# A hybrid mixer layer on one core: where the second pair's up-projection weights are prepared, which operand is finished first, and which PSUM banks the first two pairs use

## The chip, the cores and the metric

The kernel runs on one core of a Trainium2 chip. The metric is the device time of one execution in microseconds. The core has a matrix engine (PE; its weight loads are listed apart as PEld), a vector engine (DVE), a scalar engine (ACT), a general engine (POOL), which here mostly issues transfers, and a sync engine (SP), which issues transfers only. They run side by side, each through its own list of instructions in a fixed order, and wait for one another by semaphores. Matrix products are accumulated in PSUM, in banks of 512 fp32 columns; DVE and ACT read them from there.

## The reference

One layer is computed for 512 sample tokens and 128 prompt tokens, 640 in all: four token mixers with gates, an output projection, and a gated feed-forward network with a convolution over neighbouring tokens. The change concerns the step from the output projection to the network's up projection:

```
x = x + g1 * (merged @ w_o)
h = rmsnorm(x, norm2_g) * (1.0 + sc2) + sh2
x = x + g2 * conv_ffn(h, ...)

def conv_ffn(h, w_up, cw, cb, w_down):
    z = dwconv3(h @ w_up, cw, cb)
    a, g = jnp.split(z, 2, axis=-1)
    return (jax.nn.silu(g) * a) @ w_down
```

`h` is 640 x 1024, `w_up` is 1024 x 5632, `w_down` is 2816 x 1024.

## The kernel before

Every fp32 product is made of three matmuls in a faster 32-bit format. An operand x is split into a high half (ACT copies x, which rounds it) and a low half (DVE subtracts the high half from x); the product is high x high + high x low + low x high.

**The up loop.** The 5632 output columns are 22 pairs of 128 + 128 (the two halves of the gated unit). Tokens are split into two halves of 320 (`HC`), the 1024 features into two of 512. Each pair is thus a 2 x 2 block product, done in Winograd's form with seven block products in place of eight. A block product, `prod`, is twelve matmuls (4 k-tiles x 3) of 320 columns. Products are numbered 1 to 7. Each has an operand on the token side (1, 2 and 4 are blocks of h; 3, 5, 6 and 7 are sums and differences of blocks) and one on the weight side. The weight side of a pair lies in three "units": A for products 1 and 2 (plain blocks of the weight), B for 5 and 6 and the high half of 7, C for 3 and 4 and the low half of 7. B and C hold sums of weight blocks (`up_sums`, four sums of 512 columns) and one plain block, all split into high and low (`up_b`, `up_bl`, `up_c`).

`up_pair` is the loop's body. Step p runs products 6, 5 and 7 of pair p, products 4 and 3 of pair p-1, and for pairs from 4 on products 1 and 2 of pair p (`up_start`). ACT and DVE take the results out of PSUM, apply the convolution (`centre`: one ACT instruction; `taps`: two DVE multiply-adds of 641 columns), the gate, and POOL stores the result. They also prepare the weights of the next pair. For the first four pairs (`BRIDGE`) products 1 and 2 run ahead of the loop, as they need the plain blocks of h alone; meanwhile the last tokens are normalised and the sums of blocks made (`operands`).

**The passage before it.** The output projection `wo_tile(nh, kk_, w)` has two halves of 512 columns; in the first (nh = 0) four k-steps accumulate five token tiles in five banks `wo["acc"]`; in the second (nh = 1) each token tile is finished in turn, and `norm2(t)` starts: square sum on ACT, scaling on DVE, and after a delay eight transposes on PE, whose results ACT and DVE bring into the blocks of h (regions XH, XL0, XL1, X0). `up_early` runs beside the projection as a background job: it loads weight blocks of the first four pairs into regions that are free until norm2 needs them, makes unit A of pairs 0 to 3 and units B and C of pair 0, and writes those whose place is wanted later to a scratch tensor `upd` in memory. `up_back` reads them back (POOL issues it) when the projection's operands are done. Pair 1's units B and C are made in the passage itself, at step 0 of the loop.

**What sets the order.** Background jobs are Python generators. `tick` adds the planned PE time of the matmuls traced so far to a clock, and a job goes on when the time it yielded has passed (`UE`, `HD`: planned microseconds). This gives a program order. A scheduler then orders each engine's list by that priority and by when it believes the operands ready; it may put a ready instruction ahead of one that is not. `tc.keep_in_program_order` pins an instruction behind the one traced before it on the same engine. `ovec`, `oact` and `opool` pin all that goes through them while `fixed[0]` is set, which is so inside the loop (their rows carry line 148). Matmuls of the loop are not pinned.

**Where tiles live.** `region(tag, ...)` gives a named place in SBUF, used by one tile after another; the next user waits for the last access of the one before. `wp` and `rp` are rings of three places. `pg()` gives a PSUM tile of two banks (two such tiles), `pm()` one of a single bank (four). In the loop each pair's two accumulators `up[p_, "b"]` are the two halves of one `pg()` tile; pairs 2 and 3 use `pm()`.

Of the kernel before, what the change touches and what calls it, by code (L numbers as in the profile page):

```python
# [38 lines left out]
m17LH m07HL m15HL m17HL m16LH m14HH m24HL m26HL m27LH  # L39
""".split()  # L40
WARM = 100
UE = [5, 3]
NPL = 2
LOWD = ("ac", "ax", "ab", "d")
T = 640
# [22 lines left out]
def tile_step(ctx: ExitStack, tc: tile.TileContext, a: dict, outs: list, dbg=None):  # L68
# [1157 lines left out]
    def wo_tile(nh, kk_, w):  # L1226
        if (nh, kk_) == (0, 0):
            start(up_early(), 1)
            drain(lambda: "ada39" in R)
            grows["g1"] = gain_load(0, "F")  # L1230
            xr0 = region("X0", [P, 2560])
            xr1 = region("X1", [P, 2560])
            xr2 = region("G", [P, 1280])
            x2.extend([xr0[:, 0:1024], xr0[:, 1024:2048], xr1[:, 0:1024], xr1[:, 1024:2048],
                       xr2[:, 0:1024]])
            for t in range(5):
                pool.dma_start(x2[t], xsrc[t])
            g0, g1, m0 = pg(), pg(), pm()
            wo["acc"] = [m0, g0[:, 0, :], g0[:, 1, :], g1[:, 0, :], g1[:, 1, :]]
        wo[kk_] = w  # L1240
        if nh == 1 and kk_ < 3:
            return
        for t in range(5):
            m = pm() if nh == 1 else wo["acc"][t]
            for q in (range(4) if nh == 1 else (kk_,)):
                for k in (2 * q, 2 * q + 1):
                    for i, (hx, hw) in enumerate(((0, 0), (0, 1), (1, 0))):
                        mm(m, mh[k // 2][:, hx, k % 2, t * P:(t + 1) * P], wo[q][:, hw, k % 2, :],  # L1248
                           start=(k == 0 and i == 0), stop=(k == 7 and i == 2))
                    tick(0.65)  # L1250
            if kk_ < 3:
                continue
            v = 0 if t < 4 else 1
            tmp = gp.tile([P, 512], F32, tag="gt", name=nm("wt"))
            cs = slice(nh * 512, nh * 512 + 512)
            vec.tensor_tensor(tmp, m, grows["g1"][:, v, cs], ALU.mult)
# [11 lines left out]
    def norm2(t):  # L1268
# [9 lines left out]
        vec.tensor_scalar(xn, x2[t], st2[:, 8 + t:9 + t], None, ALU.mult)  # L1278
# [82 lines left out]

    upd = dram.tile([4, P, 5, 4, P], F32, name="upd")

    def up_early():
        x = region("XH", [P, 5, 8, P])
        ra, r1, r2 = x[:, 0], x[:, 3], x[:, 4]
        r3 = region("XL1", [P, 8, P])
        rb = region("H", [P, 8, P])  # L1370
        for r, p_, h in ((r2, 2, 0), (r3, 3, 0), (ra, 0, 0), (rb, 0, 1), (r1, 1, 0)):
            nc.sync.dma_start(r, a["w_up"][p_, h].rearrange("p a b c -> p (a b) c"))
        flat = lambda v: v.rearrange("p a b c -> p (a b) c")

        def part(hi, lo, v):
            act(hi, v, AF.Copy)
# [12 lines left out]
        s = x[:, 1:3].rearrange("p a b c -> p (a b) c")  # L1389
        b11, b21, b22, b12 = ra[:, 0:4], ra[:, 4:8], rb[:, 0:4], rb[:, 4:8]  # L1390
        q = [s[:, 4 * i:4 * i + 4] for i in range(4)]
        vec.tensor_tensor(q[0], b11, b12, ALU.add)
        vec.tensor_tensor(q[1], q[0], b22, ALU.add)
        vec.tensor_tensor(q[2], b12, b22, ALU.add)
        yield UE[1]
        vec.tensor_tensor(q[3], q[1], b21, ALU.add)
        b, c = [region(t, [P, 5, 4, P], F32R) for t in ("XL1", "XL0")]
        part(flat(b[:, 0:2]), flat(b[:, 2:4]), s[:, 0:8])
        part(b[:, 4], c[:, 4], q[2])
        nc.sync.dma_start(upd[2], b.bitcast(F32))  # L1400
        yield UE[1]
        for i, v in enumerate((q[3], b22)):
            part(c[:, i], c[:, 2 + i], v)
        nc.sync.dma_start(upd[3], c.bitcast(F32))
        R["early"] = True

    def up_back(p_, u, w, i, n):
        up[p_, u] = w
        pool.dma_start(w[:, 0:n], upd[i][:, 0:n])

    def up_sums(p_, r, part):
        s = sums(p_)
# [27 lines left out]
    def prod(o, p_, i, first, part=None):  # L1440

        u, ih, il = PROD[i]
        wh = up[p_, u][:, ih]
        wl = up[p_, "C" if i == 7 else u][:, il]
        xh_, xl_ = fx["x"][i]
        for k in range(4) if part is not None else ():
            for j, (w, x) in enumerate(((wl, xh_),) if part else ((wh, xh_), (wh, xl_))):
                mm(o, w[:, k, :], x[:, k, :], start=(first and not part and k == 0 and j == 0),
                   stop=(part == 1 and k == 3), skip_group_check=True)
                tick(0.147)  # L1450
        for k in range(4) if part is None else ():
            for j, (w, x) in enumerate(((wh, xh_), (wh, xl_), (wl, xh_))):
                mm(o, w[:, k, :], x[:, k, :], start=(first and k == 0 and j == 0),  # L1453
                   stop=(k == 3 and j == 2), skip_group_check=True)
            tick(0.44)

    def up_start(p_):

        if p_ == 2 or p_ == 3:
            up[p_, "b"] = [pm()[:, 0:HC], None]  # L1460
        else:
            g = pg()
            up[p_, "b"] = [g[:, 0, 0:HC], g[:, 1, 0:HC]]
        if p_ >= BRIDGE:
# [73 lines left out]
    def up_u2(p_):  # L1538

        if up[p_, "b"][1] is None:  # L1540
            up[p_, "b"][1] = pm()[:, 0:HC]
        b1 = up[p_, "b"][0]
        prod(b1, p_, 6, False)
        oact(tmp(p_ % 2), b1, AF.Copy)

    def up_pair(p_, r):
# [3 lines left out]
        inner, nx = p_ < NPAIR, n < NPAIR  # L1550
        if p_ == 0:
            up_u2(p_)
            up_sums(n, r[n], 0)
            up_sums(n, r[n], 1)
            operand3()
        if o >= 0:
            taps(o, 1)
        if q >= 0:

            oact(tmp(2), up[q, "b"][0], AF.Copy)  # L1560
            for (i0, i1, c) in S2:
                ovec.tensor_tensor(ubuf(q, 1)[:, c:c + i1 - i0], up[q, "b"][1][:, i0:i1], tmp(2)[:, i0:i1],
                                  ALU.subtract)
# [25 lines left out]
        if q >= 0:  # L1589
# [7 lines left out]
            if p_ == 1:  # L1597
                first_copy(3)
                first_sum(3)
        if inner and p_:  # L1600
# [5 lines left out]
        if nx:  # L1606
            up_b(n)
        if q >= 0:
            centre(q, 1)
        if nx:  # L1610
            up_bl(n)
        if inner:
            b1, b2 = up[p_, "b"]
# [3 lines left out]
    def operands(c0, c1):  # L1617

        if "t" not in fx:
            fx["t"] = region("X1", [P, 2, 4, HC])  # L1620
# [6 lines left out]
        def split(w, x, dma=False):  # L1627
            w = w[:, :, :, c0:c1]
            oact(w[:, 0], x, AF.Copy)
            if dma:  # L1630
                low_dma(w[:, 1], x)
            else:
                ovec.tensor_tensor(w[:, 1], x, w[:, 0].bitcast(F32), ALU.subtract)
# [512 lines left out]
```

## Time and profile before

| | |
|---|---|
| time before, median of 3 runs | 1030.13 us (1029.94 to 1030.38) |
| the profiled execution's own time | 1029.45 us |
| its span, first to last instruction | 1027.7 us |
| granted TensorE clock, mean | 0.998 |
| PE busy | 1013.2 us, 99% |
| DVE busy | 789.9 us, 77% |
| ACT busy | 537.3 us, 52% |
| POOL busy | 109.1 us, 11% |
| output projection, first and last matmul's start | 534.5 us, 591.8 us |
| products 1 and 2 of pairs 0 to 3 | 591.8 to 607.7 us |
| up loop, first product 6 | 607.7 us |

A row of the profile in order of time gives the start, the length, the engine, the line, the operation, the tile written <- the tiles read with their shapes, the count, and in brackets how long the engine was idle before and what ended it. Tile names are those of the regions: A, B and D hold operands 6, 5 and 7; E and w (the ring) hold unit B of an even and an odd pair; C and w hold unit C; XL is XL0 or XL1; g is a half of a two-bank PSUM tile, m a one-bank tile. Matmuls are pipelined: a row of twelve is 1.92 us long, but the next begins 1.76 us after it. The chain of waits lists only such steps.

### The profile page before, as it was taken

What the parts mean: (1) busy time and instruction counts of PE and PEld (TensorE: products, weight loads), DVE (VectorE), ACT (ScalarE), POOL (GpSimd) and SP (SyncE); (2) the same over time, 40 slices, a digit from 0 to 9 for tenths busy, and PEclk for the clock granted to TensorE, in tenths of its full rate; (3) what the DMA queues carried; (4) which work ended last, traced back from release to release, by engine and by line L of the source; (5) the groups of instructions that cost most, each with busy time, mean ns of one, the idle gap of its engine ahead of it and who ended that gap; (6) DMA issues with size and microseconds to landing.
All of it is one profiled execution on the core that took longest, in us unless ns stands there. A gap on an engine that the chain in (4) does not pass through costs nothing.

```text
span 1027.7 us, 18840 instructions
## 1 busy us (share of the span) xinstructions
PE 1013.2 (99%) x7620; PEld 956.9 (93%) x7620; DVE 789.9 (77%) x1299; ACT 537.3 (52%) x931; POOL 109.1 (11%) x150
## 2 busy tenths in 40 slices
PE   8999999999999999999999999999999999999997
PEld 7899989999899999999998889999999999888886
DVE  6758899679966676776868689998888887796634
ACT  6642353353545444444543477777777776633332
POOL 1000020313100000000010112111112211001101
PEclk9999999999999999999999999999999999999999
DMA  9864333598552412322177376765555669973202
GB/s 354 320 220 127 125 122 105 165 276 228 138 192 78 154 53 102 138 68 103 62 291 302 112 253 148 196 164 149 149 150 149 155 161 278 360 265 133 89 35 103
DMA packets 56311, 174.06 MB, mean 169 GB/s; under 512 B 8192, under 2 KB 15136, under 8 KB 54176
## 3 DMA queue, kind: packets, MB, share of 16 engines
q1 hardware_dynamic: 44864, 138.50, 38.6%
q0 software_dynamic: 11360, 34.36, 14.7%
q8 instruction: 60, 0.98, 0.4%
q14 instruction: 27, 0.22, 0.1%
HBM read 132.83 MB, written 22.83 MB: 151 GB/s over the span
## 4 chain that ended last, share of the span: by engine, by line
PE 96%; DMA 1%; DVE 1%; issue 1%; ACT 0%; SPq 0%; POOL 0%; POOLq 0%
PE g L1453 20%; PE g L362 17%; PE m L1108 17%; PE g L1768 8%; PE m L1768 6%; PE m L1453 5%; PE g L1121 5%; PE m L1248 3%; PE g L920 2%; PE g L1248 2%; PE m L148 2%; PE g L148 1%; PE m L526 1%; DMA A<-in_w_ada_dram 1%; PE m L851 1%; PE m L920 1%
## 5 line engine op out<-in xcount | busy, mean ns | idle before, releaser
L362 PE MATMUL g<-XH,w 128*128 128x320 f32 x704 | 170.7, 317 | 0.0
L362 PEld LDWEIGHTS g<-XH,w 128*128 128x128 f32 x704 | 120.5, 188 | 2.2 <-issue 1.2
L362 PE MATMUL g<-XL,w 128*128 128x320 f32 x352 | 109.1, 310 | 0.0
L362 PEld LDWEIGHTS g<-XL,w 128*128 128x128 f32 x352 | 66.3, 188 | 0.3 <-issue 0.2
L311 DVE TENSOR_TENSOR w<-raw,w 128x1024 fp32r<-128x1024 f32 x34 | 41.4, 1221 | 20.0 <-ACT w L310 13.8
L1108 PE MATMUL m<-XH,w 128*128 128x320 f32 x224 | 52.5, 309 | 0.0
L1768 PE MATMUL g<-w,XH 128*128 128x512 f32 (+1 forms) x216 | 47.6, 373 | 0.0
L310 ACT ACTIVATE w<-raw 128x1024 fp32r<-128x1024 f32 x34 | 35.7, 1050 | 22.7 <-PE g L1248 11.6
L1768 PEld LDWEIGHTS g<-w,XH 128*128 128x128 f32 x216 | 38.4, 188 | 7.6 <-ACT XH L1731 0.3
L148 DVE SCALAR_TENSOR_TENSOR X<-MG,p2t,X 128x641 f32<-128x641 f32 x44 | 38.9, 884 | 5.7 <-ACT X L148 4.7
L148 DVE SCALAR_TENSOR_TENSOR X<-X,p2t,X 128x641 f32<-128x641 f32 x44 | 38.8, 883 | 1.9 <-ACT X L148 1.0
L1768 PE MATMUL g<-w,XL 128*128 128x512 f32 (+1 forms) x180 | 39.8, 372 | 0.0
L1768 PE MATMUL m<-w,XH 128*128 128x512 f32 (+1 forms) x180 | 39.7, 368 | 0.0
L148 ACT ACTIVATE w<-raw 128x1024 fp32r<-128x1024 f32 (+3 forms) x46 | 38.2, 850 | 2.1 <-DMA raw<-in_w_in_dram 1.1
L1453 PE MATMUL g<-XL,C 128*128 128x320 f32 x240 | 38.6, 310 | 0.4 <-ACT MG L148 0.4
L1453 PE MATMUL g<-XL,w 128*128 128x320 f32 x240 | 38.7, 310 | 0.0
L1768 PEld LDWEIGHTS g<-w,XL 128*128 128x128 f32 x180 | 32.3, 188 | 6.5 <-DVE dt L1779 0.4
L1108 PEld LDWEIGHTS m<-XH,w 128*128 128x128 f32 x224 | 38.2, 188 | 0.0
L1453 PEld LDWEIGHTS g<-XL,C 128*128 128x128 f32 x240 | 35.9, 188 | 1.1 <-ACT MG L148 1.1
L1453 PEld LDWEIGHTS g<-XL,w 128*128 128x128 f32 x240 | 36.0, 188 | 0.5 <-ACT MG L148 0.3
L1768 PEld LDWEIGHTS m<-w,XH 128*128 128x128 f32 x180 | 31.3, 189 | 5.3
L323 ACT ACTIVATE w<-raw 128x1024 fp32r<-128x1024 f32 (+1 forms) x22 | 24.2, 1101 | 19.9 <-PE g L362 7.1
(545 smaller groups left out, 2779.1 us busy)
## 6 DMA issues: line engine op xcount, KB each, us to landing
raw<-in_w_up_dram SPq DMA_DIRECT2D x31, 512.0 KB, 4.9
raw<-in_w_gp_dram SPq DMA_DIRECT2D x21, 640.0 KB, 3.9
raw<-in_w_down_dram SPq DMA_DIRECT2D x22, 512.0 KB, 3.8
raw<-in_w_in_dram SPq DMA_DIRECT2D x19, 512.0 KB, 3.8
H<-in_w_adt_dram SPq DMA_DIRECT2D x16, 512.0 KB, 4.3
actd<-X POOLq DMA_DIRECT2D x22, 320.5 KB, 5.3
G<-in_w_up_dram SPq DMA_DIRECT2D x11, 512.0 KB, 4.9
X<-in_w_adt_dram SPq DMA_DIRECT2D x10, 512.0 KB, 4.3
```

The source lines that it names most:

```text
L148: r = f(*args, **kw)
L310: act(w[0], raw, AF.Copy)
L311: vec.tensor_tensor(w[1], raw, w[0].bitcast(F32), ALU.subtract)
L323: high = lambda: act(w[:, 0], raw, AF.Copy)
L362: mm(o, w[:, h, k0 + k, :], r(k)[:, s], start=(k == 0 and i == 0), stop=(k == kt - 1 and i == 2))
L526: mm(m[W * g:W * g + W, (i - s0) * W:(i - s0 + 1) * W], lhs, rhs, start=True, stop=True, tile_position=(64 * par, W * g))
L920: mm(o, x(kx)[:, ts], w[:, h, k, :], start=(kx == 0 and i == 0), stop=(kx == 7 and i == 2))
L1108: mm(o, w[:, k, :], x[:, k, :], start=(first and k == 0 and j == 0), stop=(k == 3 and j == 2), skip_group_check=True)
L1121: mm(pb[:, c, 0:HC], w[:, h + k, :], y[:, x, k, s], start=(k == 0 and j == 0), stop=(k == 1 and j == 2))
L1248: mm(m, mh[k // 2][:, hx, k % 2, t * P:(t + 1) * P], wo[q][:, hw, k % 2, :], start=(k == 0 and i == 0), stop=(k == 7 and i == 2))
L1453: mm(o, w[:, k, :], x[:, k, :], start=(first and k == 0 and j == 0), stop=(k == 3 and j == 2), skip_group_check=True)
L1768: mm(acc[nh][t + c0 // 256][:, 0:c1 - c0], sl[k][hx][:, t * P:(t + 1) * P], w[:, hw, k, c0:c1], start=(kk_ == 0 and k == 0 and i == 0), st ...
```

## The change

Pair 1's units B and C are made in `up_early` too, after those of pair 0, once the first half of the output projection's matmuls is traced (`R["half"]`); their three first sums are pinned. They reuse the second weight half's place `ra` for a load of pair 1's second half, go through XL1 and XL0 like those of pair 0, are written to `upd[4]` and `upd[5]`, and are read back by POOL: B ahead of pair 0's C, C (pinned) at step 0. Step 0 therefore makes no sums and step 1 no unit C. norm2 of the first token tile waits one planned microsecond longer before its transposes.

`operands` now makes operand 6 of both token parts, with its split, before operands 5 and 7 are split (`operands57`, whole width for 7); pinning begins right behind the two differences. The low half of operand 5's first part is made by DVE and no longer by an accumulating transfer. The differences lie in region F, no longer in X1. Product 6 of pair 1 comes right behind product 7 of pair 0, pinned at its first matmul, and the first accumulators are placed anew: pair 0 has the first halves of two `pg()` tiles, pair 1 the second halves. In the projection's first half the token tiles 2 and 3 swap banks. At step 1 the taps of pair 0 come behind the evacuation of product 3.

```diff
-UE = [5, 3]
+UE = [5, 3, 1]
...
-            wo["acc"] = [m0, g0[:, 0, :], g0[:, 1, :], g1[:, 0, :], g1[:, 1, :]]
+            wo["acc"] = [m0, g0[:, 0, :], g1[:, 0, :], g0[:, 1, :], g1[:, 1, :]]
...
+            if (nh, kk_, t) == (0, 3, 4):
+                R["half"] = True
...
-        yield HD[3]
+        yield HD[3] + (t == 0)
...
+        for p_, r, o in ((0, ra, rb), (1, r1, ra)):
+            b11, b21, b22, b12 = r[:, 0:4], r[:, 4:8], o[:, 0:4], o[:, 4:8]
+            while p_ and "half" not in R:
+                yield 0.5
+            for y, u, v in ((q[0], b11, b12), (q[1], q[0], b22), (q[2], b12, b22)):
+                z = vec.tensor_tensor(y, u, v, ALU.add)
+                if p_:
+                    tc.keep_in_program_order(z)
+            yield UE[1 + p_]
+            vec.tensor_tensor(q[3], q[1], b21, ALU.add)
+            if p_ == 0:
+                nc.sync.dma_start(ra, a["w_up"][1, 1].rearrange("p a b c -> p (a b) c"))
+            b, c = [region(t, [P, 5, 4, P], F32R) for t in ("XL1", "XL0")]
+            part(flat(b[:, 0:2]), flat(b[:, 2:4]), s[:, 0:8])
+            part(b[:, 4], c[:, 4], q[2])
+            nc.sync.dma_start(upd[2 + 2 * p_], b.bitcast(F32))
+            yield UE[1 + p_]
+            for i, v in enumerate((q[3], b22)):
+                part(c[:, i], c[:, 2 + i], v)
+            nc.sync.dma_start(upd[3 + 2 * p_], c.bitcast(F32))
+            yield UE[2]
...
+        elif p_ == 0:
+
+            g, h = pg(), pg()
+            up[0, "b"] = [g[:, 0, 0:HC], h[:, 0, 0:HC]]
+            up[1, "b"] = [h[:, 1, 0:HC], g[:, 1, 0:HC]]
+        elif p_ > 1:
             g = pg()
             up[p_, "b"] = [g[:, 0, 0:HC], g[:, 1, 0:HC]]
...
-        prod(b1, p_, 6, False)
+        prod(b1, p_, 6, False, pin=p_ == 1)
...
         if p_ == 0:
             up_u2(p_)
-            up_sums(n, r[n], 0)
-            up_sums(n, r[n], 1)
+            up_back(1, "C", unit(1, 2), 5, 5, True)
             operand3()
...
             oact(tmp(2), up[q, "b"][0], AF.Copy)
+            if p_ == 1:
+                up_u2(p_)
...
-        if inner and p_:
+        if inner and p_ > 1:
             up_c(p_, r[p_])
...
-            taps(q, 0)
+            if p_ > 1:
+                taps(q, 0)
+        if inner and p_ > 1:
+            up_u2(p_)
+        if q >= 0:
+
+            prod(up[q, "b"][1], q, 3, False)
+            ovec.tensor_tensor(ubuf(q, 1)[:, 1:1 + HC], up[q, "b"][1], tmp(q % 2), ALU.subtract)
             if p_ == 1:
+                taps(q, 0)
                 first_copy(3)
                 first_sum(3)
...
         ovec.tensor_tensor(t5, a21, a22, ALU.subtract)
         ovec.tensor_tensor(t6, t5, a11, ALU.subtract)
-        split(x6, t6)
-        split(x5, t5, c0 == 0)
+        if c0:
+            fixed[0] = True
         ovec.tensor_tensor(a21, a11, a21, ALU.subtract)
-        split(x7, a21)
-        ovec.tensor_tensor(t6, a12, t6, ALU.add)
+        osplit(x6[:, :, :, c0:c1], t6)
+        if not c0:
+            oact(x5[:, 0, :, c0:c1], t5, AF.Copy)
...
+    def operands57():
+        x6, x5, x7 = fx["xx"]
+        oact(x5[:, 0, :, 192:HC], fx["t"][:, 0, :, 192:HC], AF.Copy)
+        for c in (slice(0, 192), slice(192, HC)):
+            ovec.tensor_tensor(x5[:, 1, :, c], fx["t"][:, 0, :, c], x5[:, 0, :, c].bitcast(F32), ALU.subtract)
+        osplit(x7, hh[4][:, 0])
+        t6 = fx["t"][:, 1]
+        ovec.tensor_tensor(t6, hh[3][:, 1], t6, ALU.add)
...
+        up_back(1, "B", unit(1, 1), 4, 5)
...
-        r = {1: up_load(1)}
+        r = {}
         up_back(0, "C", unit(0, 2), 3, 5)
         operands(192, HC)
-        fixed[0] = True
+        operands57()
```

More of the change, by code (lines that the diff above doesn't have):

```diff
@@ L1360, in sums @@
         return fx["S"]
-    upd = dram.tile([4, P, 5, 4, P], F32, name="upd")
+    upd = dram.tile([6, P, 5, 4, P], F32, name="upd")
     def up_early():
@@ L1389, in up_early, with up_back @@
         s = x[:, 1:3].rearrange("p a b c -> p (a b) c")
-        b11, b21, b22, b12 = ra[:, 0:4], ra[:, 4:8], rb[:, 0:4], rb[:, 4:8]
         q = [s[:, 4 * i:4 * i + 4] for i in range(4)]
[L1392 to L1404, printed above, removed]
+        for p_, r, o in ((0, ra, rb), (1, r1, ra)):
[19 more added lines that the diff above has]
+            yield UE[2]
         R["early"] = True
-    def up_back(p_, u, w, i, n):
+    def up_back(p_, u, w, i, n, last=False):
         up[p_, u] = w
-        pool.dma_start(w[:, 0:n], upd[i][:, 0:n])
+        d = pool.dma_start(w[:, 0:n], upd[i][:, 0:n])
+        if last:
+            tc.keep_in_program_order(d)
     def up_sums(p_, r, part):
@@ L1438, in up_c, with prod @@
             low_dma(c[:, 2 + i].rearrange("p b c -> p (b c)"), x.rearrange("p b c -> p (b c)"))
-    def prod(o, p_, i, first, part=None):
+    def prod(o, p_, i, first, part=None, pin=False):
         u, ih, il = PROD[i]
@@ L1452, in prod @@
             for j, (w, x) in enumerate(((wh, xh_), (wh, xl_), (wl, xh_))):
-                mm(o, w[:, k, :], x[:, k, :], start=(first and k == 0 and j == 0),
-                   stop=(k == 3 and j == 2), skip_group_check=True)
+                z = mm(o, w[:, k, :], x[:, k, :], start=(first and k == 0 and j == 0),
+                       stop=(k == 3 and j == 2), skip_group_check=True)
+                if pin and k == j == 0:
+                    tc.keep_in_program_order(z)
             tick(0.44)
@@ L1595, in up_pair @@
             centre(q, 0)
-            taps(q, 0)
[L1597 to L1600, printed above, removed]
+            if p_ > 1:
+                taps(q, 0)
+        if inner and p_ > 1:
             up_u2(p_)
@@ L1605, in up_pair @@
             ovec.tensor_tensor(ubuf(q, 1)[:, 1:1 + HC], up[q, "b"][1], tmp(q % 2), ALU.subtract)
-        if nx:
+            if p_ == 1:
+                taps(q, 0)
+                first_copy(3)
+                first_sum(3)
+        if nx and p_:
             up_b(n)
@@ L1609, in up_pair @@
             centre(q, 1)
-        if nx:
+        if nx and p_:
             up_bl(n)
@@ L1619, in operands @@
         if "t" not in fx:
-            fx["t"] = region("X1", [P, 2, 4, HC])
+            fx["t"] = region("F", [P, 2, 4, HC])
             x6, x5, x7 = fx["xx"] = [region(t, [P, 2, 4, HC], F32R) for t in "ABD"]
@@ L1625, in operands, with osplit @@
         a11, a12, a21, a22 = [hh[3 + i][:, j, :, c0:c1] for i in range(2) for j in range(2)]
[L1627 to L1633, printed above, removed]
         ovec.tensor_tensor(t5, a21, a22, ALU.subtract)
         ovec.tensor_tensor(t6, t5, a11, ALU.subtract)
-        split(x6, t6)
-        split(x5, t5, c0 == 0)
+        if c0:
+            fixed[0] = True
         ovec.tensor_tensor(a21, a11, a21, ALU.subtract)
-        split(x7, a21)
-        ovec.tensor_tensor(t6, a12, t6, ALU.add)
+        osplit(x6[:, :, :, c0:c1], t6)
+        if not c0:
+            oact(x5[:, 0, :, c0:c1], t5, AF.Copy)
+    def osplit(w, x):
+        oact(w[:, 0], x, AF.Copy)
+        ovec.tensor_tensor(w[:, 1], x, w[:, 0].bitcast(F32), ALU.subtract)
+    def operands57():
[6 more added lines that the diff above has]
+        ovec.tensor_tensor(t6, hh[3][:, 1], t6, ALU.add)
     def operand3():
```

1 line of the change is left out of this document (removed).

## The prediction

> **What bounds the kernel now.** I read the page's table of engines first, then the busy time by stretch, then the chain of waits between 530 and 670 us, and last the rows of each engine in order of time through the passage from the output projection to the up loop.
>
> The page, and three stretches (columns: the stretch and its length; PE, PEld, DVE, ACT, POOL busy us with counts; granted clock; DMA share; GB/s):
>
> ```profile
> PE 1013.2 (99%) x7620; PEld 956.9 (93%) x7620; DVE 789.9 (77%) x1299; ACT 537.3 (52%) x931; POOL 109.1 (11%) x150
> ...
> 600.00:620.00 20.00, 17.91 (x116) 16.73 (x115) 18.58 (x28) 14.66 (x29) 3.93 (x11) 1.00 0.64 173
> 620.00:640.00 20.00, 20.00 (x136) 19.63 (x134) 18.40 (x27) 16.44 (x28) 3.11 (x4) 1.00 0.58 157
> 640.00:660.00 20.00, 20.00 (x139) 20.00 (x138) 19.74 (x30) 15.70 (x28) 3.69 (x6) 1.00 0.75 191
> ```
>
> PE is busy for 99% of the span, and the change leaves the number of matmuls alone. So the change can only win what PE loses waiting: 2.09 us in 600 to 620, at full granted clock. Behind it DVE is nearly full (18.40 and 19.74 of 20 us), so whatever PE wins DVE must keep up with.
>
> PE's rows in order of time (start, length, then operation), and from the chain of waits one product of twelve matmuls without a wait:
>
> ```profile
> 607.67 0.31 PE L1453 MATMUL g<-A,E 128*128 128x320 f32 x1
> 608.39 1.88 PE L1453 MATMUL g<-A,E 128*128 128x320 f32 x11 [0.42 <-DVE A L148]
> 610.80 2.19 PE L1453 MATMUL g<-B,E 128*128 128x320 f32 x12 [0.53 <-ACT MG L148]
> ...
> 615.75 1.58 PE L1453 MATMUL g<-A,w 128*128 128x320 f32 x9 [0.70 <-DVE w L148]
> 617.17 1.92 PE L1453 MATMUL g<-XL,C 128*128 128x320 f32 x12
> ...
> 619.68 2.03 PE L1453 MATMUL g<-XL,C 128*128 128x320 f32 x12 [0.44 <-ACT MG L148]
> ...
> 625.06 1.92 PE L1453 MATMUL m<-A,E 128*128 128x320 f32 x12
> ...
> 634.70 0.41 PE L1453 MATMUL m<-A,w 128*128 128x320 f32 x1
> ...
> 650.28 1.76 PE m L1453 x12
> ```
>
> Write 6(0) for product 6 of pair 0. From the start of 6(0) at 607.67 to that of 6(2) at 625.06 PE runs eight products: 17.39 us, where 8 x 1.76 = 14.08 would do. Four waits, each with its restart, cost 3.31 us. That is all there is to win here, 0.32%: (a) the low half of operand 6; (b) an evacuation by ACT, before 5(0); (c) the low half of pair 1's unit B, before most of 6(1); (d) an evacuation by ACT, before 3(0).
>
> **The change part by part.**
>
> *Wait (a), operand 6 first.* These are the rows of DVE and ACT that now lead to it, and give the lengths (512, 768 or 1280 columns):
>
> ```profile
> 604.92 0.68 DVE L148 TENSOR_TENSOR X<-X,XL 128x512 f32<-128x512 f32 x1
> 605.52 0.95 DVE L148 TENSOR_TENSOR X<-XL,X 128x768 f32<-128x768 f32 x1
> 606.39 0.95 DVE L148 TENSOR_TENSOR D<-X,D 128x768 fp32r<-128x768 f32 x1
> 607.26 0.48 DVE L148 TENSOR_TENSOR MG<-m,s 128x320 f32<-128x320 f32 x1
> 607.66 0.68 DVE L148 TENSOR_TENSOR A<-X,A 128x512 fp32r<-128x512 f32 x1
> ...
> 613.08 1.48 DVE L148 TENSOR_TENSOR XL<-X,XL 128x1280 fp32r<-128x1280 f32 x1
> ...
> 606.35 0.69 ACT L148 ACTIVATE A<-X 128x512 fp32r<-128x512 f32 x1
> ...
> 610.64 1.27 ACT L148 ACTIVATE XL<-X 128x1280 fp32r<-128x1280 f32 x1
> ```
>
> Between the sum at 604.92 and the low half at 607.66 DVE does two pieces of operands 3 and 7, which the change puts behind. The sum ends at 605.60, ACT's high half (0.69) at 606.3, the low half (0.68) at 607.0, or 607.4 with the 0.48 sum between. PE's second matmul needs it at 607.82: (a) goes. Next in line: operand 5's two low halves, 0.95 + 0.68 (one was a transfer), to 609.0, needed at 609.6; operand 7 whole, 1.48, to 610.4, needed at 611.3; the last sum, 1.48, then ACT's 1.27, then operand 3's low half, 1.48, to about 614.7, needed at 616.6. Each has 0.6 us or more of cover.
>
> *Waits (b) and (d), the banks.* In (d) PE restarts 0.05 us after ACT's second copy out of the other half of the same PSUM pair, the 0.50 us row below (two copies), ends at 619.63:
>
> ```profile
> 610.31 0.44 ACT L148 ACTIVATE MG<-g 128x320 f32<-128x320 f32 x1
> ...
> 619.13 0.50 ACT L148 ACTIVATE MG<-g 128x192 f32<-128x192 f32 x2 [1.82 <-PE g L1453]
> ```
>
> In (b) it is the row at 610.31, ending at 610.75, 0.05 before PE. I take this for a dependency on the whole tile of two banks. The change gives pair 0 one half of each of two tiles and pair 1 the other halves. Then 5(0) and 3(0) write beside halves last read long before, and the same copies are covered by a product of 1.76 us. Both go. [...]
>
> *Wait (c), pair 1's units in the output projection.* Leaving the passage: four sums (0.68 each, as other rows of 512 columns), low halves of 1.8 us (as pair 3's, further below), ACT's copies, POOL's two accumulating transfers. (c) goes, and 6(1) is pinned behind 7(0). The work lands in the projection's second half, behind the row at 564.78, which DVE's sums are pinned to:
>
> ```profile
> 564.78 1.22 DVE L311 TENSOR_TENSOR w<-raw,w 128x1024 fp32r<-128x1024 f32 x1
> 567.56 0.69 DVE L1256 TENSOR_TENSOR wt<-m,F 128x512 f32<-128x512 f32 x1 [1.56 <-PE m L1248]
> ...
> 571.03 0.75 DVE L1278 TENSOR_SCALAR C<-X,st 128x1024 f32<-128x1024 f32 x1 [0.69 <-POOL st L305]
> ...
> 574.84 1.04 PE L1290 MATMUL m<-cst,C 128*128 128x128 f32 x8
> ...
> 563.20:568.70 5.50, 5.50 (x25) 4.49 (x25) 3.63 (x5) 1.06 (x1) 0.00 (x0) 1.00 0.26 91
> 568.70:574.80 6.10, 6.10 (x28) 5.02 (x27) 2.56 (x5) 1.50 (x3) 0.56 (x1) 1.00 0.24 93
> ```
>
> Added on DVE: seven of 0.68 and one of 1.22, 6.0 us, or 5.4 as successive rows overlap by 0.08; the two stretches leave 5.4 us idle. Even if all of it went ahead of the evacuation at 567.56, that would start at 571.4, 3.8 late, and the normalised rows end at 575.6; PE transposes them at 574.84 plus the two ticks of 0.65 that the longer yield adds in the plan, 576.1. Cost nothing, with 0.5 us left in the worst case; past that each us goes to PE. The split also writes to XL1, which the transposes' copies then overwrite. Two such writes landed 6.3 and 8.7 us after their issue:
>
> ```profile
> DMA to landing us min/median/max: 6.3/7.5/8.7
> ```
>
> Issued near 568.7 the first lands between 575.0 and 577.4, for copies from about 576.6 (half the transposes' 1.04 later): late by 0.8 at most, and PE needs the banks only at later transposes. I take 0. On SP the extra load waits for DVE's read of its place, and the two writes for DVE's low halves; behind them stand stores of x2 and prefetches, wanted much later. Pair 1's two loads fall away.
>
> *The reads back.* POOL gets two more of 1280 KB. Pair 1's B is queued ahead of pair 0's C. Issues and landings now (the third and fourth on this queue), and the bandwidth meanwhile:
>
> ```profile
> L1409 POOL DMA_DIRECT2D E<-upd x1: 990/990/990, 590.5 to 590.5; - x1
> ...
> DMA to landing us min/median/max: 11.5/11.5/11.5
> ...
> L1409 POOL DMA_DIRECT2D C<-upd x1: 568/568/568, 600.2 to 600.2; - x1
> ...
> DMA to landing us min/median/max: 7.5/7.5/7.5
> ...
> 590.00:602.00 12.00, 12.00 (x83) 11.64 (x82) 8.33 (x15) 9.15 (x26) 2.79 (x11) 1.00 0.95 334
> ```
>
> The DMA engines are 95% busy, so the transfers wait on each other. E lands at 602.0 and C, the same size, at 607.7, 5.7 later. At the stretch's 334 GB/s 1.31 MB takes 3.9 us. One more ahead of C puts C at 611.6 to 613.4; 7(0) needs its low half at 611.5 and nothing covers it. Cost 0 to 1.9; I take 0.2, the fast end, because the accumulating transfer at 605.8, which shares C's time now, is gone. [...]
>
> *What is late next: DVE.* Rows at the start of pair 2 (two multiply-adds; a sum; pair 2's, then pair 3's B, low halves):
>
> ```profile
> 620.68 1.89 DVE L148 SCALAR_TENSOR_TENSOR X<-MG,p2t,X 128x641 f32<-128x641 f32 x2 [1.39 <-ACT X L148]
> 622.67 0.49 DVE L148 TENSOR_TENSOR MG<-m,s 128x320 f32<-128x320 f32 x1
> 623.08 0.48 DVE L148 TENSOR_TENSOR X<-g,MG 128x320 f32<-128x320 f32 x1
> 623.48 1.21 DVE L148 TENSOR_TENSOR E<-F,E 128x1024 fp32r<-128x1024 f32 x1
> ...
> 633.43 1.82 DVE L148 TENSOR_TENSOR w<-F,w 128x1024 fp32r<-128x1024 f32 x2
> ```
>
> Without waits 3(0) ends at 618.2 and 7(1) at 621.75, 3.31 earlier than now. DVE must then subtract 3(0) (0.48, from 618.4), do two multiply-adds (1.89), the sum (0.40 net) and only then E's low half: from 621.1 to 622.3, 2.4 earlier than now. 6(2) wants it at 622.0: 0.35 lost with the restart. From there DVE has no idle time before 634, so pair 3's B comes 2.4 earlier, too. Today 6(3)'s third matmul starts at 634.70, just behind it (633.43 + 1.22); so PE is held to a gain of about 2.4 there: another 0.55 lost.
>
> Sum: 3.31 - 0.35 - 0.55 - 0.2 = 2.2 us. The profiled execution took 1029.45 (span 1027.7), the median is 1030.13, 0.7 above. 1029.45 becomes 1027.25, and on the median's scale 1027.9.
>
> **The rivals.**
>
> *PE keeps it all.* The compiler's order may fill both handovers with other ready products, as it now runs 6(2) before 4(1). For it: 6(2) now has 0.4 us in hand. Against: at 634.70 there is none. Gain 3.3: 1026.8.
>
> [...]
>
> *Pair 0's C is late.* The slow rate, 5.7 us each, with little relief: 1.2 lost at 7(0). Gain 1.0 to 1.2, 1029.0.
>
> *Slower: the two C units share.* If pair 1's C, issued right behind pair 0's, is moved beside it and pair 1's B, all three transfers (3.93 MB) end together: at 3.9 to 5.7 us each between 613.7 and 619.1, in the middle 616.4. 7(0) then stands 4.9 us: 2.4 - 4.9, slower by 2.5, 1032.6. It loses from a landing past 613.9 on, and by 0.2% past 616. Against it: E, with two transfers ahead of it, took 11.5 us, and C, with one nearly done, 7.5: served in turn, it seems.
>
> **How the numbers follow.** 0.2% (2.06 us) is about what a measurement here can tell from no change. My forecast, DVE setting the gain, 0.48, with 1.6 to 2.7 us of gain; 0.29 of this lies above 2.06 and 0.19 below. PE keeps all 0.19. Late C 0.14, banks 0.06, shared C units 0.06, other new waits 0.07 (0.04 within 0.2%, 0.03 slower). Faster 0.29 + 0.19 = 0.48; same 0.19 + 0.14 + 0.06 + 0.04 = 0.43; slower 0.06 + 0.03 = 0.09. The range runs from the full gain, 1026.6, to a gain of 0.4, 1029.7, and leaves some 0.15 out. The likeliest case alone: 1027.4 to 1028.5.
>
> **What would show it.** Right: no wait of PE before 618 except some tenths at 7(0); then waits of PE for DVE (E, w) or ACT between 621 and 634; E's low half 2.4 us earlier, DVE without idle behind it. Wrong: a DMA releasing PE at 7(0) by over 1 us; PE still restarting behind ACT's copies before 5(0) or 3(0); PE waiting at the transposes between 575 and 590; or pair 2 without any wait.

## The result, and the profile after

The changed kernel takes 1028.84 us (median of 18 runs, 1027.65 to 1031.06) beside 1030.24 us for the kernel before (18 runs, 1029.39 to 1032.81): a ratio of 0.9983, 95% interval 0.9975 to 0.9990. In a later measurement, beside the experiments below, it took 1028.78 us (8 runs) against 1031.67 us (15 runs): 0.9968, interval 0.9956 to 0.9981. So the change wins 1.4 us in the first measurement and 2.9 in the second. Both intervals lie below 1, so there is a gain; its size is known to about 1 us only. The profiled execution took 1028.79 us, its span is 1026.9 us.

The page and the stretches of the changed kernel (length, then busy time and instructions of PE, PEld, DVE, ACT, POOL, then PE's granted clock, the DMA engines' share, GB/s). This trace runs 1.58 us late against the one of before when the up loop begins, for a reason told further below:

```profile
PE 1013.4 (99%) x7620; PEld 957.8 (93%) x7620; DVE 792.3 (77%) x1300; ACT 535.5 (52%) x927; POOL 106.2 (10%) x149
```

```profile
600.00:620.00 20.00, 20.00 (x141) 19.99 (x140) 16.77 (x23) 12.11 (x25) 1.36 (x9) 1.00 0.68 274
620.00:640.00 20.00, 19.32 (x128) 18.57 (x127) 19.06 (x30) 15.76 (x28) 3.67 (x5) 1.00 0.45 123
```

The loss of 2.09 us in 600 to 620 is gone, and 0.68 us of it comes back in 620 to 640, where DVE is now busy for 19.06 of 20 us. PE's rows in order of time:

```profile
609.25 1.92 PE L1464 MATMUL g<-A,E 128*128 128x320 f32 x12
611.01 1.92 PE L1464 MATMUL g<-B,E 128*128 128x320 f32 x12
...
613.06 0.31 PE L1464 MATMUL g<-D,C 128*128 128x320 f32 x1
...
614.53 1.92 PE L1464 MATMUL g<-A,w 128*128 128x320 f32 x12
616.29 3.68 PE L1464 MATMUL g<-XL,C 128*128 128x320 f32 x24
...
623.62 0.46 PE L1464 MATMUL m<-B,E 128*128 128x320 f32 x2
624.02 2.02 PE L1464 MATMUL g<-XL,w 128*128 128x320 f32 x12
...
630.99 0.57 PE L1464 MATMUL m<-D,E 128*128 128x320 f32 x2 [0.25 <-ACT MG L148]
...
634.04 0.41 PE L1464 MATMUL m<-A,w 128*128 128x320 f32 x1 [0.43 <-DVE w L148]
...
647.70 1.92 PE L1464 MATMUL g<-A,E 128*128 128x320 f32 x12
```

All four old waits are gone: 6(0), 5(0), 7(0), 6(1), 4(0) and 3(0) follow each other from 609.25 to 619.81 at 1.76 us each. Three places remain: 6(2), from 623.33 on, breaks off after its second matmul and other products are put ahead (a restart at 624.02, 0.21 us with the next matmul); 7(2) waits at 630.99 for a copy of ACT (0.53 us with the restart); 6(3) waits at 634.04 for DVE (0.75 us with the restarts). Together 1.49 us; found by taking the usual 0.147 us between starts of matmuls from the distances between them.

One measure frees all of this from what goes on elsewhere in the program: the time from the first matmul of 6(0) to the first of 6(4), which is the same work in every kernel here. The row of before that ends it:

```profile
648.36 1.92 PE L1453 MATMUL g<-A,E 128*128 128x320 f32 x12
```

Before it is 648.36 - 607.67 = 40.69 us, after 647.70 - 609.25 = 38.45: 2.24 us won. Another 0.16 us is won in the projection's first half (matmul by matmul, the lag of one trace behind the other falls from 1.74 to 1.58 us there), which every trace with the new order of the accumulators shows and none with the old. In all 2.40 us.

What holds PE back now, on DVE and ACT:

```profile
620.42 1.88 DVE L148 SCALAR_TENSOR_TENSOR X<-MG,p2t,X 128x641 f32<-128x641 f32 x2
622.40 0.49 DVE L148 TENSOR_TENSOR MG<-m,s 128x320 f32<-128x320 f32 x1
622.81 1.22 DVE L148 TENSOR_TENSOR E<-F,E 128x1024 fp32r<-128x1024 f32 x1
...
632.77 1.82 DVE L148 TENSOR_TENSOR w<-F,w 128x1024 fp32r<-128x1024 f32 x2
...
628.14 1.14 ACT L148 ACTIVATE C<-raw 128x512 fp32r<-128x512 f32 x2
...
629.69 0.93 ACT L148 ACTIVATE X<-MG,p2t 128x641 f32<-128x641 f32 x1
630.52 0.42 ACT L148 ACTIVATE MG<-m 128x320 f32<-128x320 f32 x1
```

E's low half starts at 622.81, which is 621.23 on the clock of before (623.48 there). The copy that frees the sums of 6(2), at 630.52, stands in ACT's queue behind the copies of a unit and behind pair 1's centre row; PE restarts 0.05 us after its end.

### The profile page after: what moved, and what is told of

It reads as the page before. It is cut to its first block, busy times and chain, and to the rows that moved or that the text cites. A ratio compares the mean times of both kernels' runs of the same rounds, so it can differ in the third digit from the quotient of the medians.

```text
span 1026.9 us, 18833 instructions
## 1 busy us (share of the span) xinstructions
PE 1013.4 (99%) x7620; PEld 957.8 (93%) x7620; DVE 792.3 (77%) x1300; ACT 535.5 (52%) x927; POOL 106.2 (10%) x149
## 4 chain that ended last, share of the span: by engine, by line
PE 96%; DMA 1%; ACT 1%; DVE 1%; issue 1%; SPq 0%; POOL 0%; POOLq 0%; DVEq 0%; ACTq 0%
PE g L1464 19%; PE g L362 17%; PE m L1108 17%; PE g L1795 8%; PE m L1795 6%; PE g L1121 5%; PE m L1464 4%; PE m L1248 3%; PE g L920 2%; PE g L1248 2%; PE m L148 2%; PE g L148 1%; PE m L526 1%; PE m L1459 1%; DMA A<-in_w_ada_dram 1%; PE m L851 1%
## 5 line engine op out<-in xcount | busy, mean ns | idle before, releaser
L1108 PE MATMUL m<-XL,w 128*128 128x320 f32 x112 | 34.6, 309 | 0.0
```

## The experiments

All times in this part are the distance from 6(0) to 6(4), unless called otherwise, since it can be compared between single executions. The three parts of the change are called units (pair 1's units made early), operand (product 6's operand first, the differences' place and the transfer that goes) and banks.

**Everything but the banks.** Pairs 0 and 1 get one tile of two banks each again:

```diff
-        elif p_ == 0:
-            g, h = pg(), pg()
-            up[0, "b"] = [g[:, 0, 0:HC], h[:, 0, 0:HC]]
-            up[1, "b"] = [h[:, 1, 0:HC], g[:, 1, 0:HC]]
-        elif p_ > 1:
+        else:
             g = pg()
```

> The changed kernel with one part undone: pairs 0 and 1 each have both accumulators in one two-bank PSUM tile again, as before; the rest of the change stays. Measure: from the start of product 6 of pair 0 to the start of product 6 of pair 4 PE needs 40.69 us in the kernel before (607.67 to 648.36) and 38.45 in the changed one (609.25 to 647.70). Theory (a write to one half of the tile waits for the read of the other half): PE stands again behind ACT's copies, before 5(0) and before 3(0), some 0.7 us each with the restart; DVE then comes later, too: 39.5 to 39.9. Rival (the new places win nothing, the waits went with the operands and units): no wait of PE for ACT before 4(1), 38.4 to 38.6.

Measured: 40.16 us, outside both ranges. PE's rows, and a row of ACT:

```profile
613.15 2.02 PE L1464 MATMUL g<-B,E 128*128 128x320 f32 x12 [0.53 <-ACT MG L148]
...
620.29 0.75 PE L1464 MATMUL g<-B,w 128*128 128x320 f32 x4
621.04 2.02 PE L1464 MATMUL g<-XL,C 128*128 128x320 f32 x12
...
627.24 1.73 PE L1464 MATMUL m<-A,E 128*128 128x320 f32 x10 [0.66 <-DVE E L148]
...
632.87 2.02 PE L1464 MATMUL g<-XL,w 128*128 128x320 f32 x12 [0.67 <-ACT MG L148]
...
620.49 0.50 ACT L148 ACTIVATE MG<-g 128x192 f32<-128x192 f32 x2 [1.26 <-PE g L1464]
```

The wait for ACT before 5(0) is back with the very 0.53 us of before, so the rival falls. Before 3(0), PE again starts 0.05 us after ACT's copies out of the other half of the tile end (620.49 + 0.50, then 621.04), but four matmuls of 5(1) fill most of that wait, and only 0.26 us is lost there, not the 0.7 of the theory. The banks are worth 1.71 us beside the other two parts, because waits for DVE (in 6(2)) and ACT (before 3(1)) further on grow with it.

**The operand alone**, with the differences kept in X1 as before:

```diff
-        split(x6, t6)
-        split(x5, t5, c0 == 0)
...
+        osplit(x6[:, :, :, c0:c1], t6)
+        if not c0:
+            oact(x5[:, 0, :, c0:c1], t5, AF.Copy)
```

> The kernel before with one part of the change alone: operand 6 of both token parts finished first, then 5, 7 and 3. Same measure, 40.69 before. Theory (DVE's list is the pace: pair 1's unit B is made behind the operands, and their sum of work stays): wait (a), 0.42 us, goes, and wait (c) before 6(1), 0.70, grows by about as much: 40.4 to 40.9. Rival (each wait is worth its own length): 40.0.

Measured: 43.12 us, outside both. PE's row, and a stretch right behind it (the third number from the end is the granted clock):

```profile
619.53 2.38 PE L1453 MATMUL g<-A,w 128*128 128x320 f32 x9 [2.09 <-DVE w L148]
```

```profile
620.00:623.40 3.40, 3.40 (x15) 3.40 (x14) 3.04 (x7) 0.94 (x2) 1.76 (x2) 0.50 0.55 92
```

DVE now has operand 5's low half to do, which was a transfer, and comes to pair 1's unit B later, while PE comes to 6(1) earlier: it waits 2.09 us at 6(1) instead of 0.70. Then the clock falls to half for 3.41 us, which costs another 1.54 (0.12 us on each matmul). Without that it would be 41.58, still slower than before. So the operand's part loses by itself.

**Units alone:**

```diff
+        for p_, r, o in ((0, ra, rb), (1, r1, ra)):
+            b11, b21, b22, b12 = r[:, 0:4], r[:, 4:8], o[:, 0:4], o[:, 4:8]
...
+            up_back(1, "C", unit(1, 2), 5, 5, True)
...
+        up_back(1, "B", unit(1, 1), 4, 5)
```

> The kernel before with another part alone: units B and C of pair 1 made during the output projection and read back, operands and banks as before. Same measure, 40.69 before. Theory: wait (c) goes, 0.97 us with its restart, (a), (b) and (d) stay as they are, since what they wait for does not depend on pair 1's units: 39.6 to 39.9. Rival (the read back of pair 1's B ahead of pair 0's C delays C, or the added work delays the transposes): a wait of PE for a DMA at 7(0) or for DVE or ACT between 575 and 595, 40 to 42.

Measured: 43.77 us, outside both ranges. The rival's wait for a DMA came, far larger, and at 5(0) in place of 7(0). PE's row, the rows of POOL, and how long the transfer into B took:

```profile
619.42 1.84 PE L1464 MATMUL g<-B,E 128*128 128x320 f32 x11 [3.09 <-DMA B<-X]
...
599.88 0.93 POOL L1418 DMA_DIRECT2D w<-upd  x1
...
604.28 0.53 POOL L1418 DMA_DIRECT2D C<-upd  x1 [3.19 <-PE g L1459]
604.80 0.54 POOL L1418 DMA_DIRECT2D w<-upd  x1
609.84 1.33 POOL L148 DMA_DIRECT2D B<-X  x1 [4.50 <-ACT B L148]
```

```profile
DMA to landing us min/median/max: 9.4/9.4/9.4
```

The low half of operand 5 is made by an accumulating transfer on POOL's queue, and the three reads of units are issued ahead of it. It lands 9.4 us after its issue; before, 5.2 us.

**Units and banks**, the operands as before:

```diff
+        elif p_ == 0:
+            g, h = pg(), pg()
+            up[0, "b"] = [g[:, 0, 0:HC], h[:, 0, 0:HC]]
+            up[1, "b"] = [h[:, 1, 0:HC], g[:, 1, 0:HC]]
```

(added to the one above)

> Pair 1's early units and the new placing of the banks, with the operands of products 5 to 7 made as before (the low half of operand 5 by an accumulating transfer on POOL's queue). Measure: from the first matmul of 6(0) to the first of 6(4), 40.69 us before, 38.45 us after. Theory (that transfer now stands behind three reads of units and lands some 9 us after its issue, where it took 5.2 us before): the PE wait of 3.09 us at 5(0), seen with the units alone, stays at 2.8 to 3.5 us: 41.5 to 43.2 us. Rival (the waits with the units alone came from the banks): 38.5 to 39.5 us.

Measured: 46.88 us. PE's row, and two stretches behind it with the granted clock third from the end:

```profile
618.20 3.30 PE L1464 MATMUL g<-B,E 128*128 128x320 f32 x11 [2.98 <-DMA B<-X]
```

```profile
620.00:623.40 3.40, 2.87 (x11) 2.47 (x11) 1.12 (x3) 0.44 (x1) 0.00 (x0) 0.50 0.00 0
623.40:627.70 4.30, 4.30 (x18) 4.30 (x17) 2.17 (x5) 1.70 (x4) 0.00 (x0) 0.50 0.28 81
```

The wait for the transfer stays (2.98 us), as the theory had it, and here the clock stands at half for 10.24 us, some 4.0 us by the distances of the matmuls. Without that it would be about 42.9 us, inside the theory's range; with it the run is outside both.

**Banks alone** (the same edit, made to the kernel before):

> The kernel before, with the new placing of the sums in the banks of pairs 0 and 1 alone. Measure: from the first matmul of 6(0) to the first of 6(4), 40.69 us before, 38.45 us after. Theory (the waits are chained): the two waits for ScalarE, 0.53 us and 0.44 us, vanish, but pair 1's unit B is as late as before on VectorE, so PE only comes earlier to 6(1) and the 0.70 us wait there grows to about 1.5 us; only the second wait with its restart (0.71 us) is won: 39.8 to 40.2 us. Rival (each wait is worth itself): both are won with their restarts, 0.95 and 0.71 us: 38.9 to 39.2 us.

Measured: 39.76 us, within 0.04 of the theory's range, far from the rival's. The two waits are not worth their own length:

```profile
613.21 1.85 PE L1453 MATMUL g<-B,E 128*128 128x320 f32 x11 [0.47 <-DMA B<-X]
...
617.61 2.02 PE L1453 MATMUL g<-XL,C 128*128 128x320 f32 x12 [0.79 <-ACT X L148]
```

The wait for ACT before 5(0) is replaced by one for the transfer into B (0.47 us), and a new one for ACT stands before 4(0). The theory had seen unit B as the next in line; it was these. Before 3(0) PE still restarts 0.05 us after a copy by ACT (at 621.92; the copy runs from 621.43 for 0.44 us): it is the copy of 6(1)'s sums, which now lie in the other half of 3(0)'s tile. So the wait again goes with the tile of two banks.

**Banks and operand, units as before** (the two edits above together):

> The changed kernel with pair 1's units made after the output projection, as before; the operand of product 6 and the banks stay as changed. Same measure. Theory (the early units carry the gain of the other two parts): VectorE now makes the operands' subtractions and pair 1's sums in one row, so pair 1's unit B comes at about 619 us, as in the run with the operand's part alone, and 6(1) waits 2.5 to 3 us: 40.6 to 41.0 us, and 1.6 us more if the clock drops to half for 3.41 us behind that wait. Rival (the banks and the operand carry the gain): 38.4 to 39.0 us.

The differences are in X1 here, and step 1 has the order of before. Measured: 40.61 us, the theory's number, but by another way, so it was reached by luck. Rows of PE, DVE and ACT:

```profile
618.24 2.02 PE L1453 MATMUL g<-XL,C 128*128 128x320 f32 x12 [2.88 <-ACT X L148]
...
616.18 1.49 DVE L148 TENSOR_TENSOR XL<-X,XL 128x1280 fp32r<-128x1280 f32 x1
...
617.75 0.44 ACT L148 ACTIVATE X<-g 128x320 f32<-128x320 f32 x1 [1.08 <-issue]
```

PE does not wait for unit B but for ACT's copy out of the sums, and that starts 0.08 us after DVE has ended operand 3's low half (616.18 + 1.49 = 617.67); with the banks alone it is the same 0.08 us (617.04 and 617.12). Both use X1: the copy goes there, and the differences of which operand 3 is made lie there. In the changed kernel they lie in F, which is free only because pair 1's sums are no longer made there at this time. That X1 is the cause is read from these rows; it wasn't tried by itself.

The eight combinations, in us of the distance, in brackets without the half-clock stretches:

```
none            40.69     banks                    39.76
operand         43.12 (41.58)   operand, banks     40.61
units           43.77     units, banks             46.88 (42.9)
units, operand  40.16     all three                38.45
```

The two runs of the last line also hold the rest of the change, which the other six lack: 6(1) pinned behind 7(0), the new order of step 1, the differences in F and the projection's new accumulators. So these are not three parts alone, and what the pin and the order of step 1 are worth by themselves was not tried. That the operand's part and the units need one another does not rest on the table alone: the rows above show the wait that each brings without the other.

**Less work on DVE.** The changed kernel without the taps of pair 0's first half (this part of the output is then missing):

```diff
             if p_ == 1:
-                taps(q, 0)
                 first_copy(3)
```

> The changed kernel without two of DVE's multiply-adds (1.88 us): the neighbouring tokens' part of the convolution for the first half of pair 0 is left out. Same measure, 38.45 in the changed kernel. Theory (DVE sets the pace from 620 to 634): the low halves for 6(2) and 6(3) come 1.9 us earlier, as does ACT's list behind the gate, and PE's waits there (0.25 and 0.43, with restarts some 1.3 us) go: 37.1 to 37.3. Rival (the handover of PSUM between ACT and PE sets it, not DVE's load): 38.2 to 38.5.

Measured: 37.27 us, as the theory had it. DVE:

```profile
621.12 1.22 DVE L148 TENSOR_TENSOR E<-F,E 128x1024 fp32r<-128x1024 f32 x1 [0.16 <-ACT E L148]
...
631.65 1.82 DVE L148 TENSOR_TENSOR w<-F,w 128x1024 fp32r<-128x1024 f32 x2
```

1.88 us less on DVE make E's low half 1.7 us earlier, and PE wins 1.18 us; of the 1.49 us of waiting 0.31 is left, all restarts. So DVE's load does set what the change wins.

**The same work on DVE, in another order**: taps of pairs 0 and 1 behind the next pair's units B, and 6(2) earlier. (Pair 3's first sum is then written over pair 0's row before the taps read it: the same instructions, with other data in pair 0's first half.)

```diff
-            if p_ == 1:
+            if p_ in (1, 2):
                 up_u2(p_)
...
             up_bl(n)
+        if p_ in (1, 2):
+            taps(q, 0)
```

> The changed kernel with VectorE's taps of pairs 0 and 1, first half, queued behind the subtractions for units B of the next pair, and product 6 of pair 2 behind the copy that frees its sums; all work is done. Same measure. Theory (what is left of waiting, at 6(2), 7(2) and 6(3), about 1.5 us with restarts, comes from the order on VectorE and ScalarE alone): 37.1 to 37.5 us, and a time 1.0 to 1.4 us below that of the changed kernel. Rival (VectorE is full from 617 to 635 us, the wait only moves to the next pair): 38.2 to 38.6 us, and the same time.

Measured: 38.51 us, and 1027.94 us in time (7 runs; 0.9965 of the kernel before in the second measurement, 0.9952 to 0.9977, where the changed kernel has 0.9968, 0.9956 to 0.9981, so the two times can't be told apart): the rival. E's low half comes in time, but PE then waits for the next things:

```profile
634.17 0.70 PE L1464 MATMUL m<-A,w 128*128 128x320 f32 x3 [0.33 <-DVE w L148]
...
646.61 2.02 PE L1464 MATMUL m<-XL,w 128*128 128x320 f32 x12 [0.32 <-ACT X L148]
```

What is put behind one unit delays another; 1.5 us of waiting remain, as in the changed kernel. Less work on DVE helped, this other order of it did not; no version here beats the changed kernel with all its work done.

**6(2) and its copy earlier, nothing else:**

```diff
-            if p_ == 1:
+            if p_ in (1, 2):
                 up_u2(p_)
```

> The changed kernel with product 6 of pair 2, and the ScalarE copy of its sums, queued right behind the copy that frees the sums of pair 1, as pair 1's already is; VectorE's order stays. Same measure. Theory (the waits are chained: the 0.53 us wait for ScalarE at 7(2) goes, but the wait for VectorE's unit B at 6(3) grows by as much): 38.2 to 38.5 us. Rival (the ScalarE wait is worth itself with its restart): 37.7 to 37.9 us.

Measured: 39.60 us, 1.15 worse than the changed kernel, which neither had. Rows of ACT, DVE and PE:

```profile
627.04 0.44 ACT L148 ACTIVATE MG<-m 128x320 f32<-128x320 f32 x1 [1.89 <-PE m L1464]
627.50 1.28 ACT L148 ACT_TABLE_LOAD   x1
628.80 0.74 ACT L148 ACTIVATE X<-X 128x641 f32<-128x641 f32 x1
...
635.11 1.81 DVE L148 TENSOR_TENSOR w<-F,w 128x1024 fp32r<-128x1024 f32 x2
...
636.38 0.41 PE L1464 MATMUL m<-A,w 128*128 128x320 f32 x1 [1.55 <-DVE w L148]
```

The copy is now ahead of the gate of pair 0 in ACT's queue, and ACT stands 1.89 us until PE has made 6(2). The table load and the gate come after it, DVE's product with the gate after that, and then unit B of pair 3. So the copy's late place in ACT's queue, 0.53 us at 7(2) in the changed kernel, was the cheaper of the two.

**Both kernels once more**, unchanged:

> The changed kernel once more, beside the one above. Same measure, 38.3 to 38.6 us. Theory (the change is worth 2.4 us, and what differs from that in the times is a half-clock stretch of 3.41 us behind the PE pause at 138 us, which comes in some runs of either kernel, and starts that differ by some tenths): runs at the same mean clock differ by 1.9 to 2.4 us between the kernels. Rival (the change is worth only the 1.4 us by which the medians differed): they differ by 1.2 to 1.6 us at the same clock too.

Measured: 38.45 us, the same to 0.01. Of the times neither number held: runs at the same mean clock, to three digits, differ by 2.9 to 3.6 us between the kernels in this measurement (medians 1030.21 and 1027.06 at 0.998, 1031.67 and 1028.05 at 0.997, 1033.15 and 1030.26 at 0.996). The mean clock is a rough sorting, though: it also counts a half-clock stretch at the end of the execution, 4.5 us long in the trace of after and 3.3 in that of before.

> The kernel before once more, profiled. Same measure, 40.6 to 40.8 us by every theory. [...]

Measured: 40.71 us, and the half-clock stretch of 3.41 us behind the pause at 138 us shows. The stretch from 138.4 to 141.8 us, in the trace of before, of after, and of before once more:

```profile
138.40:141.80 3.40, 3.40 (x25) 3.40 (x25) 3.37 (x7) 2.94 (x4) 0.09 (x1) 1.00 0.27 101
```

```profile
135.00:138.40 3.40, 2.26 (x137) 1.88 (x126) 3.02 (x8) 0.27 (x1) 0.00 (x0) 1.00 0.20 41
138.40:141.80 3.40, 3.40 (x14) 3.40 (x14) 3.37 (x7) 2.90 (x4) 0.00 (x0) 0.50 0.35 125
```

```profile
138.40:141.80 3.40, 3.40 (x19) 3.34 (x20) 3.04 (x5) 2.46 (x4) 0.00 (x0) 0.50 0.34 130
```

It is no part of the change: before has it in one execution and not in the other.

## Why the prediction was right, and where it was not

The forecast was 1027.9 us, a gain of 2.2 on the profiled execution's scale, with DVE setting it. The traces show 2.40 in all and 2.24 in the passage, and the mechanism is the one forecast: the low half of pair 3's unit B starts at 632.77, which is 631.19 on the clock of before, 2.24 us ahead of 633.43, and that is the passage's gain. The time was 1028.84, inside the range, and 0.34 above the upper end of the likeliest case's own range. The medians' gain of 1.40 us is also below the 1.6 to 2.7 of that case and below the 2.06 us from which on the forecast called it faster (0.48, its largest chance); it lies in the part that had 0.43. By its steps:

- Wait (a), (b), (c), (d) go: right, all four, each by the operation named. (b) comes back with the banks alone taken away, at 0.53 us, and so does the handover of (d), for 0.26 us; so it was the tile of two banks. The case that the banks are not the cause, which had 0.06, falls with it.
- The projection's added work on DVE costs nothing: right. DVE's eight pieces stand from 566.58 to 572.03, the evacuation follows at 571.95, and PE's transposes start at 577.79 with no wait.
- Pair 0's C late at 7(0), 0.2 us: it cost 0. It was issued at 601.79 and landed after 9.1 us at 610.9 (rows below the list), and its first matmul ran at 613.06 with 2.1 us to spare. On the clock of before 610.9 is 609.3, ahead of the forecast's 611.6 to 613.4: three reads in a row, now without the accumulating transfer among them, landed 3.3 to 3.75 us apart, less than the 3.9 taken. The rivals of a late C and of two C units sharing their time fall, too: the two landed 3.7 us apart, in turn. At 3.3 to 3.75 us for 1.31 MB that is 350 to 400 GB/s, above the 334 taken.
- 6(2) waits for E's low half, 0.35 us: right in kind. E's low half starts at 621.23 on the clock of before (forecast 621.1); it cost 0.21, because PE took 5(2) and 4(1) in between.
- 6(3) waits for pair 3's B, 0.55 us: right in kind, 0.75 measured.
- Put at nothing: the ACT wait at 7(2), 0.53 us. The forecast named a wait for ACT there as possible, but its sum followed only DVE behind the two handovers; ACT's copy of 6(2) stands behind the copies of a unit.
- Not costed: restarts of PE in the trace of before between 627 and 635, 0.42 us, which the new order does not have, and the order of the accumulators, 0.16 us. These two cover what the ACT wait took: 3.31 + 0.42 + 0.16 - 1.49 = 2.40. That the sum came within 0.2 us of this is in part luck: terms left out on both sides, and 0.2 for a late C that cost nothing, happen to cancel.
- The rival that PE keeps all (1026.8) is refuted by the same 1.49 us. The run with less work on DVE shows why it could not be so: take 1.88 us off DVE and the 1.18 come.
- The step from the profiled execution's scale to the median's failed: 0.7 us was added, but the changed kernel's profiled execution (1028.79) lies 0.05 below its median. The 1029.45 us of the trace of before is an execution without the half-clock stretch at 138 us, which costs 1.5 us (3.41 us in which a matmul of the loop's size starts every 0.267 us, not 0.147). Of thirteen traces of all kernels eleven have it, at mean clocks of 0.992 to 0.997; the two without, of before and of the run with less work on DVE, are at 0.998. A second pause of PE differs, too: between 200 and 300 us, far ahead of the passage, the other traces fall by 0 to 1.35 us further behind that of before (0 in the changed kernel's first trace, 0.68 in its second). So the trace of before was a quick one in both places, and a sum made on it says little about where a median of 18 runs lies: with 2.40 us won, 1030.24 would have become 1027.84; it became 1028.84 in the first measurement, and 2.89 were won in the second. These differences from one execution to the next, 1.5 and up to 1.35 us, are enough by the author's estimate to move a median by more than 1 us; that the whole difference is theirs isn't shown, since runs at the same mean clock still differ by more than 2.40 in the second measurement.

The reading of C in the changed kernel, its issue and the time to its landing:

```profile
601.79 0.53 POOL L1418 DMA_DIRECT2D C<-upd  x1 [3.19 <-PE g L1459]
```

```profile
DMA to landing us min/median/max: 9.1/9.1/9.1
```

The reason given for a small gain, that DVE follows hard behind PE, held. What the forecast didn't say is that the parts need one another: by themselves they change the distance by -0.93 (banks), +0.89 (operand) and +3.08 us (units), without half-clock stretches; the whole change, with the pin and the order of step 1, by -2.24.

## What to carry to other kernels

Before parts of a change are judged one by one, ask which place, queue or engine time each one takes from the others: here the early reads on a queue paid only with the transfer behind them gone, and giving up that transfer paid only with DVE freed by the early units. When the engine behind the bound one has no idle time, expect moved work to move the wait: the other orders tried here won nothing, and work taken off DVE did. And before an operation is put ahead in an engine's queue, ask when its input is ready: here ACT stood 1.89 us, and all that was queued behind the copy came later.

## What the runs showed of the hardware that was not expected

The granted clock stood at 0.50 in some stretches. In the changed kernel one begins at 138.41 us, 3.41 us long, behind a pause of PE of 1.14 us, and another at 1022.47 us, which lasts 4.46 us, to the end of the execution. In the operand's run one of 3.41 us begins at 620.02 us, behind the wait of 2.09 us. In the run with units and banks one of 10.24 us goes with the wait of 2.98 us.

The length of a pause does not tell by itself whether the clock falls. Between 135.0 and 138.4 us PE stood idle for 1.21 us in before once more and for 1.21 us in the run with less work on DVE: from 138.4 to 141.8 us the clock was 0.50 in the first and 1.00 in the second. In the up loop the waits of 2.09 us (operand) and 2.98 us (units and banks) came with a fall, and the longer 3.09 us (units) and the 2.88 us (banks and operand) left the clock at 1.00 from 612 to 632 us. What else counts was not shown. So a wait of PE cost only itself in two of these four runs; in the other two the half clock cost 1.54 us (operand) and some 4.0 us (units and banks) more.
